# Matmuls of one width in groups, one PSUM tile per bank, and each weight load split in one piece, in a float32 decoder layer

## The chip, the cores and the metric

The kernel runs on one core of a Trainium2 chip. The metric is device time in microseconds (us) of one execution. TensorE (PE in the profile) multiplies and accumulates into PSUM, whose eight banks hold 512 float32 columns each. VectorE (DVE) and ScalarE (ACT) work on SBUF and PSUM. SyncE (SP) issues the DMAs that bring the weights from HBM.

## The reference

One decoder layer in float32, for 256 tokens of width 2048. All six modulation vectors come from `silu(c) @ w_ada + b_ada`. The part in front is attention of two kinds; the part behind it is a gated feed-forward network with a causal convolution over tokens, 43 x 128 = 5504 wide:

```
sh1, sc1, g1, sh2, sc2, g2 = split(silu(c) @ w_ada + b_ada, 6)
h      = rmsnorm(x, norm1_g) * (1 + sc1) + sh1
proj   = h @ w_in                                  # q, k, v of 8 + 8 heads, and an indexer's q, k, weights
o_sb   = stick_breaking_attention(q_sb, k_sb, v_sb)
o_ds   = sparse attention over the 64 keys that the indexer selects
x      = x + g1 * (concat(rmsnorm(o_sb), rmsnorm(o_ds)) @ w_out)
h2     = rmsnorm(x, norm2_g) * (1 + sc2) + sh2
u      = h2 @ w_up                                 # 2048 -> 2 * 5504
uc     = conv_b + sum over i of shift(u, 2 - i) * conv_w[i]
x      = x + g2 * ((silu(gate) * val) @ w_down)    # gate, val: the halves of uc
out    = rmsnorm(x, final_norm_g)
```

## The kernel before, in words

All weights stream through SBUF once, in loads of 128 x 2048 float32 (1 MB, `load`, line 135, four `raw` buffers). Every operand of a large matmul is split in a high part, rounded to fp32r (ACT, line 145), and a low part, the difference (DVE, line 146). `split` does this in pieces of 1024 columns, two for each load; the high and the low pieces have three buffers each (tags `wh` and `wl`). A product is then high x high + high x low + low x high, in one of three helpers:

- `nat` (lines 149 to 153): the activations are stationary, three matmuls of up to 512 columns. Used for the projections A, A2 (tiles B) and V.
- `trn` (lines 161 to 165): the weights are stationary, three matmuls of 256 columns. Used for QK, O and the first eight tiles of U.
- `fold` (lines 155 to 159): the weights are stationary and the activations' two parts lie side by side, so one matmul of 512 columns with the high weights writes the two products next to each other in one bank, and one of 256 columns adds the low weights' product to the second half. Used for U from tile `G0` = 8 on and for W. The two halves are added afterwards.

The stages in order: A (`do_A`), A2, V and QK for the first half of the contraction; A and A2 for the second; attention, with V and QK of the second half among it; O (`do_O`, w_out) with the residual and its squares; r2 and `h2_make`; U (`do_U`, w_up, f = 0 to 42, each in two loads i = 0, 1, each load with gate and value, `gv`); W (w_down, 43 loads). For f < 8 the first loads of all eight are taken before the second ones, since the later half of h2 isn't there yet. Behind each f of U follows the work on uc (lines 835 to 855); behind each k of W the residual (lines 871 to 877: DVE's lines 875 and 726 read the bank).

Columns of the modulation are made on the side by `ada` (lines 213 to 218: a load, and one DVE instruction of 2048 elements at line 215) or, in five groups, by TensorE (`ada_pe`). `pump` puts them between other work by a plan written out as digits.

In U and W the PSUM pool has 4 tiles of two banks each (`banks`, line 782). For f >= 8 such a tile holds gate and value of one f; for f < 8 it holds two f (lines 795 to 797); in W it holds k and k + 1 (lines 868 to 870). The framework orders each engine's instructions by its own planning ahead of the run, keeps track of who writes and reads each tile, and places semaphore waits accordingly; `order` adds an ordering by hand (lines 801 to 804: two splits come after the last residual).

Of the kernel before, what the change touches and what calls it, by code (L numbers as in the profile page):

```python
# [10 lines left out]
F32 = mybir.dt.float32  # L11
# [43 lines left out]
def layer(ctx: ExitStack, tc: tile.TileContext, a, out):  # L55
# [9 lines left out]
    def s2(shape, dt, name):  # L65
        return wp.tile(shape, dt, name=name, tag="s2", bufs=4)
# [331 lines left out]
    def do_A(pi):  # L398
# [6 lines left out]
        for j in range(PARTS[pi]):  # L405
            k = P0[pi] + j
            need(16 + k)
            need(k)
            w = load(a["wA"][k], 2048, f"wA{k}")
            h_make(k, pi, j)  # L410
            pump()
            for p_ in range(2):
                wh, wl = split(w, p_ * 1024, 1024, f"wA{k}{p_}")
                for c in range(2):
                    for t in range(NT):
                        nat(acc[2 * p_ + c][t], hp(hh, pi, j)[:, t * P:(t + 1) * P], hp(hl, pi, j)[:, t * P:(t + 1) * P],
                            wh[:, c * 512:(c + 1) * 512], wl[:, c * 512:(c + 1) * 512], j == 0, j == PARTS[pi] - 1)
# [7 lines left out]
    def natural(pi, src, width, per_load, acc, name):  # L425

        n = PARTS[pi]
        for k0 in range(0, n, per_load):
# [3 lines left out]
            for k1 in range(0, nk, 2):  # L432
                n2 = min(2, nk - k1)
                wh, wl = split(w, k1 * width, n2 * width, f"{name}{k0}{k1}")
                for jj in range(n2):
                    j = k0 + k1 + jj
                    for t in range(NT):
                        nat(acc[t][:, 0:width], hp(hh, pi, j)[:, t * P:(t + 1) * P], hp(hl, pi, j)[:, t * P:(t + 1) * P],
                            wh[:, jj * width:(jj + 1) * width], wl[:, jj * width:(jj + 1) * width], j == 0, j == n - 1)
# [13 lines left out]
    def do_QK(pi, h):  # L453
        n = PARTS[pi]
        acc = ps(f"QK{pi}{h}", tag=ptag[0])
        if n <= 8:
            w = load(a[f"wQK_{pi}"][h], 2 * n * P, f"wQK{pi}{h}")
        for p_ in range(2):
            o = p_ * n * P
            if n > 8:  # L460
                w = load(a[f"wQK_{pi}"][h][:, o:o + n * P], n * P, f"wQK{pi}{h}{p_}")
                o = 0
            for j0 in range(0, n, 8):
                nj = min(8, n - j0)
                wh, wl = split(w, o + j0 * P, nj * P, f"wQK{pi}{h}{p_}{j0}")
                for j in range(j0, j0 + nj):
                    trn(acc[:, p_ * S:(p_ + 1) * S], hp(hh, pi, j), hp(hl, pi, j),
                        wh[:, (j - j0) * P:(j - j0 + 1) * P], wl[:, (j - j0) * P:(j - j0 + 1) * P], j == 0, j == n - 1)
# [308 lines left out]

# [175 lines left out]
```

## Time and profile before

| what | value |
| --- | --- |
| median of 3 runs | 1251.4 us (1251.29 to 1252.37) |
| the profiled execution | 1258.62 us, of which its span (first to last instruction) 1256.8 us |
| mean granted TensorE clock | 0.979 |
| TensorE matmuls | 7120, busy 93% of the span |
| TensorE weight loads | 7120, busy 81% (beside matmuls) |
| DVE | 1232 instructions, busy 70% |
| ACT | 969 instructions, busy 50% |
| DMA | 303.48 MB, mean 241 GB/s |

Busy time of TensorE contains the overlap of matmuls that follow each other, so the distance between two starts tells more than the duration of one. A line can be that of a helper: 158 and 159 are `fold`, and the tile's name (U, W) tells who called it. Idle time in front of an instruction is shown in brackets with the instruction that ended it.

### The profile page before, as it was taken

How to read it: one execution, taken by the hardware profiler on the slowest of the kernel's cores; microseconds unless marked ns; L12 is line 12 of the kernel's file. 1: busy time of each engine (PE TensorE's matmuls, PEld its weight loads, DVE VectorE, ACT ScalarE, POOL GpSimd, SP SyncE). 2: the span in 40 equal slices, each digit the busy share in tenths (PEclk: the TensorE clock that was granted, in tenths of full speed). 3: DMA queues.
4: the chain of work that ended last, by engine and by line, in shares of the span. 5: the costliest groups of instructions: out<-in, count | busy, mean ns of one | idle time of the engine just before them, and what ended most of it. 6: DMA issues, size and time to landing. Idle time of an engine off the chain costs nothing.

```text
span 1256.8 us, 17813 instructions
## 1 busy us (share of the span) xinstructions
PE 1171.3 (93%) x7120; PEld 1016.9 (81%) x7120; DVE 880.5 (70%) x1232; ACT 629.3 (50%) x969; POOL 0.2 (0%) x4
## 2 busy tenths in 40 slices
PE   4699999899999997988999999999999999999995
PEld 2478987567879997987888888888888888888885
DVE  4877787789667888756789778777777645545443
ACT  3355554466555544454555555555555543443441
POOL 0000000000000000000000000000000000000000
PEclk9799999999999998999999999999999999999998
DMA  8988989667678896844578666666665445455431
GB/s 307 365 332 303 339 331 336 231 252 277 228 293 351 298 330 258 306 165 168 181 250 316 224 226 229 215 241 224 214 225 190 179 172 192 172 175 183 179 135 67
DMA packets 43282, 303.48 MB, mean 241 GB/s; under 512 B 4928, under 2 KB 5440, under 8 KB 7232
## 3 DMA queue, kind: packets, MB, share of 16 engines
q1 hardware_dynamic: 43200, 302.35, 66.0%
q8 instruction: 55, 0.90, 0.3%
q14 instruction: 27, 0.22, 0.0%
HBM read 300.24 MB, written 2.10 MB: 241 GB/s over the span
## 4 chain that ended last, share of the span: by engine, by line
PE 82%; DVE 11%; ACT 3%; DMA 2%; issue 2%; SPq 0%; DVEq 0%; ACTq 0%
PE U L158 20%; PE W L158 13%; PE U L159 10%; PE W L159 6%; DVE wa L215 3%; PE U L165 2%; PE U L164 2%; PE U L163 2%; PE O L165 2%; PE O L163 2%; PE O L164 2%; PE QK L163 2%; PE QK L164 2%; PE QK L165 2%; DMA wa<-wa 2%; PE A L151 2%
## 5 line engine op out<-in xcount | busy, mean ns | idle before, releaser
L215 DVE SCALAR_TENSOR_TENSOR wa<-wa,scb 128x2048 f32<-128x2048 f32 x76 | 173.5, 2285 | 6.9 <-DMA wa<-wa 6.6
L847 DVE SCALAR_TENSOR_TENSOR uc<-u,par,uc 128x254 f32<-128x254 f32 (+1 forms) x140 | 58.2, 478 | 0.0
L843 ACT ACTIVATE uc<-u,par 128x256 f32<-128x256 f32 x70 | 38.2, 593 | 0.8 <-DVE u L837 0.8
L854 ACT CAST aT<-uc 128x256 fp32r<-128x256 f32 x43 | 17.4, 404 | 28.8 <-DVE uc L853 28.7
L313 ACT ACTIVATE amul<-mod,b,par 128x1 f32<-128x1 f32 x32 | 12.0, 385 | 32.2 <-DVE wa L215 32.2
L192 PE MATMUL ap<-wg,csil 128*32 128x512 f32 x160 | 26.4, 679 | 0.3 <-DVE mod L201 0.3
L855 DVE TENSOR_TENSOR aT<-uc,aT 128x256 fp32r<-128x256 f32 x43 | 18.2, 422 | 10.0 <-ACT aT L854 9.9
L837 DVE TENSOR_TENSOR u<-U,u 128x512 f32<-128x512 f32 x35 | 23.9, 684 | 0.0
L316 ACT ACTIVATE mod<-mod,par 128x1 f32<-128x1 f32 x32 | 8.6, 302 | 27.5 <-DVE wa L215 26.6
L836 ACT COPY u<-U 128x512 f32<-128x512 f32 x35 | 20.3, 580 | 0.0
L853 DVE TENSOR_TENSOR uc<-uc 128x256 f32<-128x256 f32 x43 | 18.1, 420 | 1.5 <-ACT uc L849 0.7
L849 ACT ACTIVATE uc<-uc 128x256 f32<-128x256 f32 x43 | 17.7, 411 | 1.5 <-DVE uc L847 1.5
L731 ACT ACTIVATE x2q<-x1T 128x256 f32<-128x256 f32 x15 | 6.2, 415 | 21.3 <-DVE x1T L726 21.2
L875 DVE SCALAR_TENSOR_TENSOR x1T<-W,mod,x1T 128x256 f32<-128x256 f32 x16 | 7.7, 481 | 12.0 <-PE W L159 12.0
L847 DVE SCALAR_TENSOR_TENSOR uc<-U,par,uc 128x255 f32<-128x255 f32 (+1 forms) x32 | 14.5, 477 | 1.4 <-ACT uc L843 1.2
L192 PEld LDWEIGHTS ap<-wg,csil 128*32 128x32 f32 x160 | 4.7, 120 | 10.0 <-issue 8.2
L843 ACT ACTIVATE uc<-U,par 128x256 f32<-128x256 f32 x16 | 9.0, 561 | 7.5 <-DVE uc L847 7.5
L676 ACT ACTIVATE sbt<-sbt 128x384 f32<-128x384 f32 x8 | 4.2, 524 | 14.8 <-DVE sbt L675 14.8
L562 DVE SCALAR_TENSOR_TENSOR scw<-rl,wix,scw 128x128 f32<-128x128 f32 (+1 forms) x28 | 10.4, 409 | 0.0
L545 PE MATMUL rel<-ws,qixT 64*128 64x128 f32 (+1 forms) x64 | 8.5, 345 | 2.0 <-ACT rl L550 2.0
L273 PE MATMUL cb<-ident,csil 128*128 128x128 f32 x16 | 3.6, 422 | 7.1 <-DMA ident<-ident 7.1
L197 ACT COPY rw<-ap 128x512 f32<-128x512 f32 x5 | 2.9, 586 | 14.0 <-PE ap L192 13.3
(2810 smaller groups left out, 4600.7 us busy)
## 6 DMA issues: line engine op xcount, KB each, us to landing
wU<-wU SPq DMA_DIRECT2D x86, 1024.0 KB, 4.8
wa<-wa SPq DMA_DIRECT2D x76, 1024.0 KB, 5.4
wD<-wD SPq DMA_DIRECT2D x43, 1024.0 KB, 4.6
wg<-wg SPq DMA_DIRECT2D x20, 1024.0 KB, 6.2
wA<-wA SPq DMA_DIRECT2D x16, 1024.0 KB, 6.4
wQK<-wQK SPq DMA_DIRECT2D x16, 1024.0 KB, 6.9
wO<-wO SPq DMA_DIRECT2D x16, 1024.0 KB, 6.9
xT<-xT SPq DMA_DIRECT2D x4, 512.0 KB, 5.9
```

The source lines that it names most:

```text
L151: T.matmul(pt, lhsT=xh, rhs=wh, start=first, stop=False)
L158: T.matmul(pt, lhsT=wh, rhs=x, start=first, stop=False)
L159: T.matmul(pt[:, 1, :], lhsT=wl, rhs=x[:, 0, :], start=False, stop=last)
L163: T.matmul(pt, lhsT=wh, rhs=xh, start=first, stop=False)
L164: T.matmul(pt, lhsT=wh, rhs=xl, start=False, stop=False)
L165: T.matmul(pt, lhsT=wl, rhs=xh, start=False, stop=last)
L192: T.matmul(pt[32 * j:32 * j + 32, :], lhsT=csil[:, k:k + 1].to_broadcast([P, 32]), rhs=w[:, j * 512:(j + 1) * 512], start=q == 0, stop=q == 3)
L215: i = V.scalar_tensor_tensor(out=w, in0=w, scalar=1.0, in1=scb, op0=ALU.mult, op1=ALU.mult, accum_out=mod[:, j:j + 1])
L836: A.copy(out=u, in_=acc[:, :, 1, :])
L837: V.tensor_tensor(out=u, in0=acc[:, :, 0, :], in1=u, op=ALU.add)
L843: A.activation(uc[:, gv, :], u[:, gv, :], AF.Identity, scale=par[:, PCW + 3 * i + 2:PCW + 3 * i + 3], bias=par[:, PCB + i:PCB + i + 1])
L847: V.scalar_tensor_tensor(out=uc[:, gv, sft:S], in0=u[:, gv, 0:S - sft], scalar=par[:, o:o + 1], in1=uc[:, gv, sft:S], op0=ALU.mult, op1=AL ...
```

## The change

It does four things. `fold` takes a list of steps and issues all their 512-column matmuls with the high weights first and all 256-column matmuls with the low weights after them; U and W hand it eight steps at a time. In U and W a PSUM tile is one bank (`bank`, 8 tiles): one per f for f < 8, one each for gate and value for f >= 8, one per k in W, where the residual's work is issued after the group of eight in which k ends. `split` handles a whole load of up to 2048 columns, with two buffers each for the high and the low part. To make room the tag `s2` has 3 buffers in place of 4, and the sum u has a tag of its own with 2. The two orderings by hand become one: the whole split of the first load of U comes after the last residual.

```diff
-        return wp.tile(shape, dt, name=name, tag="s2", bufs=4)
+        return wp.tile(shape, dt, name=name, tag="s2", bufs=3)
...
-    def split(w, off, n, name):
-        wh = wp.tile([P, 1024], F32R, name=name + "h", tag="wh", bufs=3)
-        wl = wp.tile([P, 1024], F32R, name=name + "l", tag="wl", bufs=3)
-        lo_[1] = A.copy(out=wh[:, 0:n], in_=w[:, off:off + n])
-        lo_[0] = V.tensor_tensor(out=wl[:, 0:n], in0=w[:, off:off + n], in1=wh[:, 0:n].bitcast(F32), op=ALU.subtract)
+    def split(w, n, name):
+        wh = wp.tile([P, 2048], F32R, name=name + "h", tag="wh", bufs=2)
+        wl = wp.tile([P, 2048], F32R, name=name + "l", tag="wl", bufs=2)
+        lo_[1] = A.copy(out=wh[:, 0:n], in_=w[:, 0:n])
+        lo_[0] = V.tensor_tensor(out=wl[:, 0:n], in0=w[:, 0:n], in1=wh[:, 0:n].bitcast(F32), op=ALU.subtract)
...
-    def fold(pt, x, wh, wl, first, last):
-        T.matmul(pt, lhsT=wh, rhs=x, start=first, stop=False)
-        T.matmul(pt[:, 1, :], lhsT=wl, rhs=x[:, 0, :], start=False, stop=last)
+    def fold(steps):
+        for pt, x, wh, _, first, _ in steps:
+            T.matmul(pt, lhsT=wh, rhs=x, start=first, stop=False)
+        for pt, x, _, wl, _, last in steps:
+            T.matmul(pt[:, 1, :], lhsT=wl, rhs=x[:, 0, :], start=False, stop=last)
...
     def do_O(acc, m, s, xh, xl):
         w = load(a["wO"][m, s], 2048, f"wO{m}{s}")
+        wh, wl = split(w, 2048, f"wO{m}{s}")
         for p_ in range(2):
-            wh, wl = split(w, p_ * 1024, 1024, f"wO{m}{s}{p_}")
             for j in range(8):
...
-    pool3 = ctx3.enter_context(tc.tile_pool(name="psC", bufs=4, space=PSUM))
+    pool3 = ctx3.enter_context(tc.tile_pool(name="psC", bufs=8, space=PSUM))
...
-    def banks(name):
-        return pool3.tile([P, 2, 2, S], F32, name=name, tag="ps", bufs=4)
+    def bank(name):
+        return pool3.tile([P, 2, S], F32, name=name, tag="ps", bufs=8)
...
         if i == 0:
-            if f >= G0:
-                uacc[f] = banks(f"U{f}")
-            elif f % 2 == 0:
-                t_ = banks(f"U{f}")
-                uacc[f], uacc[f + 1] = t_[:, 0], t_[:, 1]
+            uacc[f] = [bank(f"U{f}{gv}") for gv in range(2)] if f >= G0 else bank(f"U{f}")
         w = load(a["wU"][f, i], 2048, f"wU{f}{i}")
+        wh, wl = split(w, 2048, f"wU{f}{i}")
+        if (f, i) == (0, 0):
+            order(lo_[0], resid_i[0])
+            order(lo_[1], resid_i[1])
         for gv in range(2):
-            wh, wl = split(w, gv * 1024, 1024, f"wU{f}{i}{gv}")
-            if (f, i, gv) in ((0, 0, 1), (1, 0, 0)):
-                order(lo_[0], resid_i[0])
-                if gv == 0:
-                    order(lo_[1], resid_i[1])
+            steps = []
...
                 if f >= G0:
-                    fold(uacc[f][:, gv], x, wh[:, sl], wl[:, sl], k == 0, k == KT - 1)
+                    steps.append((uacc[f][gv], x, wh[:, sl], wl[:, sl], k == 0, k == KT - 1))
...
+            fold(steps)
...
         if f >= G0:
-            u = s2([P, 2, S], F32, f"u{f}")
-            A.copy(out=u, in_=acc[:, :, 1, :])
-            V.tensor_tensor(out=u, in0=acc[:, :, 0, :], in1=u, op=ALU.add)
+            u = wp.tile([P, 2, S], F32, name=f"u{f}", tag="u2", bufs=2)
+            for gv in range(2):
+                A.copy(out=u[:, gv, :], in_=acc[gv][:, 1, :])
+                V.tensor_tensor(out=u[:, gv, :], in0=acc[gv][:, 0, :], in1=u[:, gv, :], op=ALU.add)
...
+    wacc = {}
     for q in range(FT):
         w = load(a["wD"][:, q * 2048:(q + 1) * 2048], 2048, f"wD{q}")
+        wh, wl = split(w, 2048, f"wD{q}")
         for p_ in range(2):
-            wh, wl = split(w, p_ * 1024, 1024, f"wD{q}{p_}")
-            for j in range(8):
-                k, f = divmod((2 * q + p_) * 8 + j, FT)
-                if f == 0 and k % 2 == 0:
-                    acc = banks(f"W{k}")
-                fold(acc[:, k % 2], aT[f // 4][:, f % 4, :, :], wh[:, j * P:(j + 1) * P], wl[:, j * P:(j + 1) * P],
-                     f == 0, f == FT - 1)
+            steps, done = [], None
+            for j in range(8 * p_, 8 * p_ + 8):
+                k, f = divmod(16 * q + j, FT)
+                if f == 0:
+                    wacc[k] = bank(f"W{k}")
+                sl = slice(j * P, (j + 1) * P)
+                steps.append((wacc[k], aT[f // 4][:, f % 4, :, :], wh[:, sl], wl[:, sl], f == 0, f == FT - 1))
                 if f == FT - 1:
...
+                    done = k
+            fold(steps)
+            if done is not None:
...
```

The loops of A, A2, V and QK change in the same way as `do_O`: one `split` per load, and the same matmuls in the same order.

## Rows read from the trace of the kernel before

**Rows 1.** The page: busy time by engine, and the chain's shares by line.
```profile
PE 1171.3 (93%) x7120; PEld 1016.9 (81%) x7120; DVE 880.5 (70%) x1232; ACT 629.3 (50%) x969; POOL 0.2 (0%) x4
...
PE U L158 20%; PE W L158 13%; PE U L159 10%; PE W L159 6%; DVE wa L215 3%; PE U L165 2%; PE U L164 2%; PE U L163 2%; PE O L165 2%; PE O L163 2%; PE O L164 2%; PE QK L163 2%; PE QK L164 2%; PE QK L165 2%; DMA wa<-wa 2%; PE A L151 2%
```

**Rows 2.** Stages: length; PE, PEld, DVE, ACT, POOL busy (count); PEclk, DMA share, GB/s.
```profile
372.00:472.00 100.00, 99.15 (x814) 95.33 (x807) 82.81 (x97) 51.15 (x77) 0.00 (x0) 1.00 0.86 321
531.00:595.00 64.00, 54.50 (x405) 52.22 (x404) 39.72 (x61) 30.61 (x47) 0.00 (x0) 0.95 0.51 181
595.00:988.00 393.00, 392.73 (x2224) 340.24 (x2223) 302.05 (x414) 219.35 (x313) 0.00 (x0) 1.00 0.63 225
988.00:1243.00 255.00, 243.51 (x1379) 210.49 (x1379) 123.90 (x135) 104.72 (x120) 0.00 (x0) 1.00 0.45 161
```

**Rows 3.** Timeline of PE in U: start, duration; the first of eight pairs, twice.
```profile
801.74 0.40 PE L158 MATMUL U<-h,wU2610h 128*128 128x512 f32 x1
...
804.57 0.40 PE L158 MATMUL U<-h,wU2611h 128*128 128x512 f32 x1
```

**Rows 4.** Timeline of PE in V: eighteen steps of 512 columns lie between.
```profile
119.83 0.39 PE L153 MATMUL V<-V0140h,hl 128*128 128x512 f32 x1
...
123.91 0.39 PE L153 MATMUL V<-V0142h,hl 128*128 128x512 f32 x1
```

**Rows 5.** Timeline of PE in O: twenty-four steps of 256 columns lie between.
```profile
420.27 0.28 PE L163 MATMUL O<-osh,wO310h 128*128 128x256 f32 x1
...
423.15 0.28 PE L163 MATMUL O<-osh,wO311h 128*128 128x256 f32 x1
```

**Rows 6.** Waits from 988 to 1243 us: total us, times, longest.
```profile
PEld W L158 <- DVE x1T L726: 13.8, 8, 2.5
...
PE W L158 <- DVE x1T L726: 11.5, 8, 2.2
```

**Rows 7.** Timeline of DVE at the first of these waits.
```profile
1003.65 1.23 DVE L146 TENSOR_TENSOR wD31l<-wD,wD31h 128x1024 fp32r<-128x1024 f32 x1 [1.65 <-ACT wD31h L145]
...
1005.31 0.48 DVE L726 SCALAR_TENSOR_TENSOR x1T<-W,mod,x1T 128x256 f32<-128x256 f32 x1
```

**Rows 8.** Timeline of PE in U's second pass (tiles are named wU, f, i, gv).
```profile
531.26 0.28 PE L163 MATMUL U<-h,wU010h 128*128 128x256 f32 x1
...
538.20 0.39 PE L163 MATMUL U<-h,wU210h 128*128 128x256 f32 x1 [1.02 <-ACT wU210h L145]
...
594.86 0.40 PE L158 MATMUL U<-h,wU801h 128*128 128x512 f32 x1
```

**Rows 9.** Timelines of ACT and DVE in O.
```profile
426.15 1.05 ACT L145 CAST wO410h<-wO 128x1024 fp32r<-128x1024 f32 x1 [1.82 <-PE O L164]
...
428.50 1.22 DVE L146 TENSOR_TENSOR wO410l<-wO,wO410h 128x1024 fp32r<-128x1024 f32 x1
...
431.61 2.28 DVE L215 SCALAR_TENSOR_TENSOR wa<-wa,scb 128x2048 f32<-128x2048 f32 x1
```

**Rows 10.** The page's groups: busy us, mean ns of one, idle before and its releaser.
```profile
L215 DVE SCALAR_TENSOR_TENSOR wa<-wa,scb 128x2048 f32<-128x2048 f32 x76 | 173.5, 2285 | 6.9 <-DMA wa<-wa 6.6
L855 DVE TENSOR_TENSOR aT<-uc,aT 128x256 fp32r<-128x256 f32 x43 | 18.2, 422 | 10.0 <-ACT aT L854 9.9
L836 ACT COPY u<-U 128x512 f32<-128x512 f32 x35 | 20.3, 580 | 0.0
L847 DVE SCALAR_TENSOR_TENSOR uc<-U,par,uc 128x255 f32<-128x255 f32 (+1 forms) x32 | 14.5, 477 | 1.4 <-ACT uc L843 1.2
```

**Rows 11.** The chain in order of time at two starts, O and U: start, us.
```profile
389.36 0.95 ACT wO200h L145
390.33 1.24 DVE wO200l L146
...
474.60 1.23 DVE wU100l L146
```

**Rows 12.** Line 215 alone from 20 to 531 us: busy us, two records each.
```profile
20.00:531.00 511.00, 137.47 (x120) 0.96 0.81 300
```

More of the change, by code (lines that the diff above doesn't have):

```diff
@@ L411, in do_A @@
             pump()
[L412 to L417, printed above, removed]
+            wh, wl = split(w, 2048, f"wA{k}")
+            for c in range(4):
+                sl = slice(c * 512, (c + 1) * 512)
+                for t in range(NT):
+                    nat(acc[c][t], hp(hh, pi, j)[:, t * P:(t + 1) * P], hp(hl, pi, j)[:, t * P:(t + 1) * P], wh[:, sl],
+                        wl[:, sl], j == 0, j == PARTS[pi] - 1)
         for g in range(4):
@@ L431, in natural @@
             pump()
[L432 to L439, printed above, removed]
+            wh, wl = split(w, nk * width, f"{name}{k0}")
+            for jj in range(nk):
+                j = k0 + jj
+                for t in range(NT):
+                    nat(acc[t][:, 0:width], hp(hh, pi, j)[:, t * P:(t + 1) * P], hp(hl, pi, j)[:, t * P:(t + 1) * P],
+                        wh[:, jj * width:(jj + 1) * width], wl[:, jj * width:(jj + 1) * width], j == 0, j == n - 1)
     def do_A2(pi):
@@ L455, in do_QK @@
         acc = ps(f"QK{pi}{h}", tag=ptag[0])
-        if n <= 8:
-            w = load(a[f"wQK_{pi}"][h], 2 * n * P, f"wQK{pi}{h}")
+        w = load(a[f"wQK_{pi}"][h], 2 * n * P, f"wQK{pi}{h}")
+        wh, wl = split(w, 2 * n * P, f"wQK{pi}{h}")
         for p_ in range(2):
[L459 to L468, printed above, removed]
+            for j in range(n):
+                sl = slice((p_ * n + j) * P, (p_ * n + j + 1) * P)
+                trn(acc[:, p_ * S:(p_ + 1) * S], hp(hh, pi, j), hp(hl, pi, j), wh[:, sl], wl[:, sl], j == 0, j == n - 1)
         dst = qk[h // 4]
@@ L701, in do_O @@
         w = load(a["wO"][m, s], 2048, f"wO{m}{s}")
+        wh, wl = split(w, 2048, f"wO{m}{s}")
         for p_ in range(2):
-            wh, wl = split(w, p_ * 1024, 1024, f"wO{m}{s}{p_}")
             for j in range(8):
-                trn(acc[:, p_ * S:(p_ + 1) * S], xh[:, j, :], xl[:, j, :], wh[:, j * P:(j + 1) * P],
-                    wl[:, j * P:(j + 1) * P], s == 0 and p_ == 0 and j == 0, s == 1 and p_ == 1 and j == 7)
+                sl = slice((8 * p_ + j) * P, (8 * p_ + j + 1) * P)
+                trn(acc[:, p_ * S:(p_ + 1) * S], xh[:, j, :], xl[:, j, :], wh[:, sl], wl[:, sl],
+                    s == 0 and p_ == 0 and j == 0, s == 1 and p_ == 1 and j == 7)
     acc = [ps(f"O{m}", tag="acc") for m in range(4)]
@@ L776, in layer @@
     ctx3 = ExitStack()
-    pool3 = ctx3.enter_context(tc.tile_pool(name="psC", bufs=4, space=PSUM))
-    psum_pool[0] = (pool3, {"ps": 4})
+    pool3 = ctx3.enter_context(tc.tile_pool(name="psC", bufs=8, space=PSUM))
+    psum_pool[0] = (pool3, {"ps": 8})
     ptag[0] = "ps"
-    def banks(name):
-        return pool3.tile([P, 2, 2, S], F32, name=name, tag="ps", bufs=4)
+    def bank(name):
+        return pool3.tile([P, 2, S], F32, name=name, tag="ps", bufs=8)
     aT = []
@@ L807, in do_U @@
                 x = h2[k // 4][:, k % 4, :, :]
-                sl = slice(j * P, (j + 1) * P)
+                sl = slice((8 * gv + j) * P, (8 * gv + j + 1) * P)
                 if f >= G0:
-                    fold(uacc[f][:, gv], x, wh[:, sl], wl[:, sl], k == 0, k == KT - 1)
+                    steps.append((uacc[f][gv], x, wh[:, sl], wl[:, sl], k == 0, k == KT - 1))
                 else:
```

12 lines of the change are left out of this document (7 added, 5 removed).

## The prediction

> **What bounds the kernel now.** The shares of busy time come first [rows 1]: TensorE is busy 93% of the 1256.8 us, and the chain that ended last lies on it for most of its length, above all in `fold` (lines 158 and 159, in U and W). So the next view is the table by stage, where the question is how much of each stage TensorE does *not* work [rows 2]. Three stretches differ. From 595 to 988 us (U, tiles f = 8 to 42) it is busy without a gap, so only shorter matmuls can help. From 988 to 1243 (W) it lacks 11.5 us, and from 531 to 595 (second half of U's first eight tiles) 9.5 us, at a mean clock of 0.95; there waits can be removed. From 372 to 472 (O), as in the other stages of `nat` and `trn`, it is full, and DVE with 82.8 us of 100 stands close behind it: here a change of DVE's or ACT's order can only hurt.
>
> Last comes the distance from start to start of matmuls, since busy time hides their overlap. In `fold` a pair of 512 and 256 columns takes 2.83 us / 8 = 0.3538 us [rows 3]. Where only 512 columns follow each other it is 4.08 / 18 = 0.2267 us each [rows 4]; where only 256, 2.88 / 24 = 0.1200 us [rows 5]. One of each would be 0.3467 us. The pair costs 7 ns more than its two halves in uniform rows (6 to 7, as the stamps are rounded).
>
> **The change part by part.**
>
> **1. Grouping.** `fold` issues 8 wide matmuls, then 8 narrow ones. There are 35 x 32 = 1120 pairs in U and 43 x 16 = 688 in W, 1808 together. If the 7 ns belong to the alternation, seven of eight disappear: 1808 x 7/8 x 6.6 ns = 10.5 us. Nothing lies beside them: in this stretch TensorE has no gap [rows 2]. Bounds: 0, if the price stays with the widths and not the order, and 12.8 (1808 x 7.1 ns, no transition left). I take 10.5, since [rows 4, 5] are the same types, with a weight load ahead of every matmul, as in `fold` (7120 of each on the page). The Trainium skill (TensorE: Matmul & The Clock Gate, Back-to-back issue gap) gives a matmul a gap that depends on its own columns alone, N/2.4 + 2.5 ns, and no price for a change of width; by it, called an estimate, a pair is 325 ns in either order and the term is 0. The cadences above lie higher and the pair is not the sum of its halves, so the trace doesn't bear that out; what it would do here is rival A.
>
> **2. One tile per bank in W.** Before, k and k+1 share a tile of two banks. TensorE waits 8 times, 11.5 us in all, for DVE's line 726 [rows 6], always at the first matmul of an odd k, which goes to the other bank of a tile that DVE is still reading. Before DVE gets there it does a split already queued, then the two reads, 0.48 us each [rows 7]. With a tile per k and 8 of them this wait has no cause: the bank that k+1 gets was emptied several k earlier. W holds 688 x 0.3538 = 243.4 us of matmuls in 255, which gives the same: 11.5. With the restart of the pipeline I take 12.0 (bounds 11.5 and 13.8, the wait of the weight loads). What is late next: nothing near; each k lasts 43 x 0.35 = 15 us and its two reads may fall anywhere in it. The tail behind the last k stays as it is.
>
> **3. One tile per bank in U, f < 8.** Here f and f+1 share a tile; TensorE takes f = 2, 4, 6, 8 ahead of f = 1, 3, 5, 7, whose split isn't made yet when it comes [rows 8] (f = 2 there; three more of the kind, at 4, 6 and 8). From 531.26 to 594.86 us there are 16 pieces of 24 x 0.12 = 2.88 us and one of 2.83 in `fold`, 48.9 us, in 63.6: 14.7 us are lost, part of it in waits like the 1.0 us at wU210h, part at the lowered clock that follows some of them (mean 0.95 of the stretch). With a tile per f the order is f = 0, 1, 2, ... and no matmul waits for a reader. DVE needs per f a split of 2.3 us and about 2.8 us of small work behind U (four at line 847 of 0.48, two like line 855 of 0.42 [rows 10]), under the 5.76 us of TensorE, but not by much. I take 13 (bounds 8, with half a microsecond or more of new wait per f, and 14.7).
>
> **4. One split of 2048.** An ACT copy of 1024 takes 1.05 us, a DVE subtraction 1.22 [rows 9]; of 2048, DVE 2.28 (line 215, the same number of elements), ACT 1.05 + 2 x (1.05 - 0.58) = 1.99 by the slope from 512 [rows 9, 10]. Per load ACT saves 0.1 and DVE 0.15 us; TensorE sets the pace, so that is worth nothing. Two things are paid.
>
> *At each start*, where TensorE stands ready and the split is the last to come, the first matmul pair could go 1.05 + 1.22 us after the copy began; now 1.99 + 2.28: +2.0 us, less where TensorE waits for something else too. In `fold` it is nothing: the 8 wide matmuls (1.8 us) need the copy alone and cover most of the subtraction. Starts in `nat` and `trn` that the chain shows: the first loads of A and its last ones (wA60), the end of A's second part, V and QK behind attention, wO200, and U's first load (the last two stand in [rows 11]). In U it is worse, as the whole split of load 0 must now come behind the last residual, and DVE's small steps to r2 queue behind 2.28 us in place of 1.23. I set A 1.5, A's second part 1.5, V and QK together 1.5, O 2, U 2: 8.5 us (bounds 2, if other waits cover them, and 14, seven full ones).
>
> *In steady running* the reserve shrinks. A buffer is free when TensorE has left it (the copy's releaser in [rows 9]). With three of 1024 it is needed again after 2 x 2.88 us and takes 1.05 + 1.22: 3.5 us in hand. With two of 2048 it is needed after 5.76 and takes 4.3: 1.5 us (1.1 in `nat`, whose load lasts 24 x 0.2267 = 5.44). What can eat it is line 215, 2.3 us in one piece on DVE, 60 of them up to 531 us [rows 12] beside 68 loads. DVE is idle while ACT copies, so a line 215 whose data has landed begins there, ahead of the subtraction, and ends in time; one that starts just before the copy ends makes TensorE wait 2.3 - 1.5 = 0.8 us. I take 2 us, two or three such (bounds 0 and 12). In `fold` the copy's buffer is free 8 x 0.12 us before the load ends and the subtraction's result is needed 1.8 us into the next: 4 us in hand, no cost. The Trainium skill (Perfetto Trace Analysis, Optimizing Scalar/DVE Operations) speaks against this part: where ScalarE and VectorE aren't saturated but cause bubbles elsewhere, it advises breaking instructions up. The start rows agree; no row here shows it yet for steady running.
>
> **5. The rest** is set at nothing. s2 with 3 buffers and u2 with 2 of its own: U's chain had four for u and uc, now two and three. Loads: a raw buffer is held for 4.3 us instead of one piece of TensorE and a split; SP's queue keeps its order. If either cover fails it shows as waits of ACT or SP, inside the bounds of part 4.
>
> **The sum**, against the profiled execution: -10.5 - 12.0 - 13 + 8.5 + 2 = -25.0 us, 1256.8 to 1231.8 of span. The profiled execution itself took 1258.6; the median of the runs is 1251.4, and I take the difference as the same there: 1226.4.
>
> **The rivals.**
>
> A. *Alternation isn't the cause* of the 7 ns, grouping moves nothing: 1226.4 + 10.5 = 1237. For it: no row shows a group inside `fold`. Against: two uniform cadences whose sum is less than the pair.
>
> B. *The tiles change nothing*: the waits in W and U come from reads as such, a matmul into any bank waits behind DVE. Then 12 and 13 us stay: 1251.4. Against it: all 8 waits stand at odd k and none at even k, whose tile is new.
>
> C. *Slower: two buffers starve TensorE.* Place: A to O and U's first tiles, DVE between ACT's copy and its subtraction. Price: 0.9 us for each line 215 that lands late enough to start there (0.8 and the restart). With 40 of the 60 it is 36 us, in place of the 2: 1226.4 + 34 = 1260. It makes the kernel slower from about 30 on (25 + 2 = 27 us / 0.9). For it: O's loads run at 321 GB/s [rows 2], and line 215 waits for its data already, 6.6 us in all [rows 10]. Against it: DVE's idle time, while ACT copies, now lies just where a line 215 fits.
>
> **How the numbers follow.** Forecast 0.70; A 0.15; B 0.05; C 0.07; 0.03 for something unseen, a third of it on each side and within. The forecast's own bounds: best -12.8 - 13.8 - 14.7 + 2 = -39; all at once is unlikely, -38 gives 1213. Worst without C: -5 - 11.5 - 8 + 14 + 4 = -6.5, 1245; I end at 1243. That range, 1213 to 1243, takes in A and leaves out B, C and little else. Faster by over 0.2% (2.5 us, about what a measurement of this kernel can tell from no change): forecast, A and a third of the unseen, 0.86. Same, B and a third: 0.06. Slower, C and a third: 0.08.
>
> **What would show it.** Grouping: starts 0.227 us apart in rows of 8 on line 158's successor, then 0.120. W: no wait of TensorE for DVE's reads, 43 x 16 pairs in 239 us. U: f in order and a clock of 1.00 between the first pass and f = 8. Splits: 1.99 and 2.28 us, TensorE's new waits for ACT or DVE at the starts named, and in O a subtraction ending some 1.4 us ahead of its first use. Wrong would be a cadence of 0.354 in groups (A), waits for DVE's reads that remain (B), or gaps of about 0.8 us load after load between 100 and 530 us (C).

## The result, and the profile after

The changed kernel takes 1233.6 us (median of 4 runs, 1232.9 to 1235.3), beside 1251.4 for the kernel before in the same batch of runs. The ratio is 0.9862, with a 95% interval of 0.9845 to 0.9879: 17.8 us faster. The forecast was 1226.4 with a range of 1213 to 1243; the time lies inside, 7 us above the forecast. The profiled execution took 1232.9 us, 1230.9 of it span, 25.9 less than that of before. The forecast for the span was 1231.8. That this agrees so closely is partly luck, as the terms below show.

The page of the kernel after, the line that answers to the first of [rows 1]:

```profile
PE 1159.2 (94%) x7120; PEld 1017.6 (83%) x7120; DVE 871.2 (71%) x1078; ACT 605.6 (49%) x815; POOL 0.2 (0%) x4
```

As many matmuls as before, 12.1 us less busy time, and 154 instructions fewer each on DVE and ACT. The stages say more. The kernel after by stage, columns as in [rows 2] (length; PE, PEld, DVE, ACT, POOL busy; PEclk, DMA share, GB/s): O, U's first pass, U's second pass, the rest of U, W.

```profile
372.00:478.00 106.00, 97.06 (x774) 94.33 (x773) 78.82 (x81) 44.09 (x62) 0.00 (x0) 0.95 0.75 275
478.00:540.00 62.00, 51.81 (x404) 51.01 (x403) 50.10 (x61) 27.66 (x38) 0.00 (x0) 0.89 0.72 265
540.00:586.00 46.00, 45.74 (x381) 45.53 (x380) 35.32 (x47) 27.25 (x36) 0.00 (x0) 1.00 0.58 205
586.00:977.00 391.00, 391.00 (x2241) 344.09 (x2241) 309.84 (x387) 220.32 (x282) 0.00 (x0) 1.00 0.63 229
977.00:1218.00 241.00, 241.00 (x1386) 212.18 (x1384) 117.90 (x93) 95.18 (x77) 0.00 (x0) 1.00 0.47 170
```

The last three are full: the second pass, 63.6 us before with one piece of `fold` (2.8) in it, takes 46.6 (539.78 to 586.42, start of its first matmul to that of `fold`), and W, 255.0 before, takes 240.1. The first of them is not: in O, which was full in [rows 2], TensorE now lacks 9 us of 106, and its clock is 0.95: from 400.4 to 410.7 us, around the waits at rsbb and osh below, the granted clock is 0.50, the lower of its two levels (1.2 GHz).

The groups stand as intended. Timeline of PE in the kernel after (start, duration; rows with a count join matmuls that follow each other):

```profile
800.56 1.12 PE L162 MATMUL U<-h,wU270l 128*128 128x256 f32 x8
801.51 2.00 PE L160 MATMUL U<-h,wU270h 128*128 128x512 f32 x8
803.35 0.76 PE L162 MATMUL U<-h,wU270l 128*128 128x256 f32 x5
```

From 800.56 to 801.51 eight narrow ones go by in 0.95 us, from 801.51 to 803.35 eight wide ones in 1.84: 2.79 for eight pairs, where [rows 3] give 2.83.

Waits of PE in the kernel after, 372 to 540 us (total us, times, longest):

```profile
PE r2b L129 <- DVE r2y L126: 5.9, 1, 5.9
PE rsbb L129 <- DVE rsby L126: 4.7, 1, 4.7
PE O L166 <- ACT osh L640: 2.8, 1, 2.8
PE U L166 <- DVE g L305: 2.7, 1, 2.7
```

Before, the same stretch has neither a wait at rsbb nor one at osh, and the one at r2b is 1.7 us. From 586 to 1218 us TensorE waits for nothing at all; the eight waits of [rows 6] are gone.

So where did it go? The table gives, for the kernels of the experiments below too, the start of TensorE's first or last matmul of a stretch, in us from the start of the span. "Heads" is the last matmul of the stick-breaking heads, "rsb" the first one of their norm.

| | before | p12 | after | e6 | e5 | e7 | e8 | e9 |
| --- | --- | --- | --- | --- | --- | --- | --- | --- |
| A, second part, first | 170.2 | 170.8 | 172.5 | 168.6 | 175.8 | 173.2 | 168.9 | 169.8 |
| attention, last `av` | 290.0 | 290.3 | 295.1 | 293.2 | 297.0 | 294.6 | 291.9 | 291.7 |
| heads, last | 379.9 | 376.4 | 389.8 | 373.9 | 391.9 | 389.5 | 373.7 | 372.2 |
| rsb | 383.3 | 379.9 | 398.1 | 394.6 | 400.1 | 391.8 | 382.9 | 381.4 |
| O, last | 472.0 | 468.4 | 478.2 | 476.3 | 480.3 | 474.5 | 464.2 | 462.7 |
| U, first | 479.0 | 475.4 | 490.2 | 487.6 | 488.3 | 486.6 | 472.5 | 471.0 |
| U, first pass, last | 531.1 | 523.7 | 539.7 | 536.0 | 539.8 | 536.5 | 523.1 | 521.8 |
| W, first | 988.3 | 961.0 | 977.5 | 973.3 | 977.6 | 974.4 | 960.4 | 957.6 |

From before to after: 6.2 us are lost up to O's end and 5.1 more up to U's first matmul; the first pass of U gains 2.8, from there to W it is 19.3 (14.1 of it in the second pass), in W 14.9. Two executions with one order of instructions differ by some us before U (e5 and after are the same up to there, and lie 3.3 us apart at A's second part), so the early rows are read with that in mind.

### The profile page after: what moved, and what is told of

Its sections match the earlier page's. It is cut to its first block, busy times and chain, and to the rows that moved or that the text cites. A ratio compares the mean times of both kernels' runs of the same rounds, so it can differ in the third digit from the quotient of the medians.

```text
span 1230.9 us, 17235 instructions
## 1 busy us (share of the span) xinstructions
PE 1159.2 (94%) x7120; PEld 1017.6 (83%) x7120; DVE 871.2 (71%) x1078; ACT 605.6 (49%) x815; POOL 0.2 (0%) x4
## 4 chain that ended last, share of the span: by engine, by line
PE 85%; DVE 8%; ACT 3%; DMA 3%; issue 2%; SPq 0%; DVEq 0%; ACTq 0%
PE U L160 21%; PE W L160 13%; PE U L162 11%; PE W L162 7%; PE O L168 2%; PE O L167 2%; PE O L166 2%; PE U L168 2%; PE U L166 2%; PE U L167 2%; PE QK L168 2%; PE QK L166 2%; PE QK L167 2%; PE A L152 2%; PE A L153 2%; PE A L151 2%
## 5 line engine op out<-in xcount | busy, mean ns | idle before, releaser
L839 DVE SCALAR_TENSOR_TENSOR uc<-u,par,uc 128x255 f32<-128x255 f32 (+1 forms) x140 | 67.4, 482 | 31.1 <-ACT uc L835 27.8
L835 ACT ACTIVATE uc<-u,par 128x256 f32<-128x256 f32 x70 | 42.1, 602 | 87.8 <-DVE u L829 87.8
L828 ACT COPY u<-U 128x256 f32<-128x256 f32 x70 | 25.6, 366 | 56.1 <-PE U L162 56.1
L829 DVE TENSOR_TENSOR u<-U,u 128x256 f32<-128x256 f32 x70 | 29.2, 417 | 0.0
L721 DVE SCALAR_TENSOR_TENSOR x1T<-O,mod,xT 128x256 f32<-128x256 f32 x16 | 7.0, 478 | 13.0 <-PE O L168 13.0
L151 PE MATMUL A<-wA0h,hh 128*128 128x512 f32 x8 | 3.7, 536 | 9.0 <-ACT hh L311 9.0
```

The lines of the kernel that those rows point to most:

```text
L151: T.matmul(pt, lhsT=xh, rhs=wh, start=first, stop=False)
L828: A.copy(out=u[:, gv, :], in_=acc[gv][:, 1, :])
L829: V.tensor_tensor(out=u[:, gv, :], in0=acc[gv][:, 0, :], in1=u[:, gv, :], op=ALU.add)
L835: A.activation(uc[:, gv, :], u[:, gv, :], AF.Identity, scale=par[:, PCW + 3 * i + 2:PCW + 3 * i + 3], bias=par[:, PCB + i:PCB + i + 1])
L839: V.scalar_tensor_tensor(out=uc[:, gv, sft:S], in0=u[:, gv, 0:S - sft], scalar=par[:, o:o + 1], in1=uc[:, gv, sft:S], op0=ALU.mult, op1=AL ...
```

## The experiments

The theories: mine, that the four terms add up as in the sum; rivals A, B and C; and, once the result was known, three places in which the split of 2048 could cost what steady running doesn't.

**The parts one by one.** p1 is the grouping on the kernel before, with tiles of two banks kept; p2 is the tile per bank, with the old `fold`; p3 is the split of 2048 with its two buffers, `s2` and `u2`; p12 is p1 and p2 together.

```diff
 p1, in W:
+                    wacc[k] = banks(f"W{k}") if k % 2 == 0 else wacc[k - 1]
...
+            fold(steps)
+            if done is not None:
 p2:
-            if f >= G0:
-                uacc[f] = banks(f"U{f}")
-            elif f % 2 == 0:
-                t_ = banks(f"U{f}")
-                uacc[f], uacc[f + 1] = t_[:, 0], t_[:, 1]
+            uacc[f] = [bank(f"U{f}{gv}") for gv in range(2)] if f >= G0 else bank(f"U{f}")
...
-                if f == 0 and k % 2 == 0:
-                    acc = banks(f"W{k}")
+                if f == 0:
+                    acc = bank(f"W{k}")
 p3:
-        wh = wp.tile([P, 1024], F32R, name=name + "h", tag="wh", bufs=3)
-        wl = wp.tile([P, 1024], F32R, name=name + "l", tag="wl", bufs=3)
+        wh = wp.tile([P, 2048], F32R, name=name + "h", tag="wh", bufs=2)
+        wl = wp.tile([P, 2048], F32R, name=name + "l", tag="wl", bufs=2)
```

p1: 

> Grouping alone on the kernel before: splits of 1024 with three buffers and the tiles of two banks stay. The theory (the price of the alternation is real, but part of it returns at the first five wide matmuls of each group: 27 ns in each of 226 groups) expects 6.7 us less, 1244.7, and groups of 1.85 us wide and 0.95 us narrow. The prediction's own term was 10.5 us less, 1240.9. Rival A (the order doesn't matter) expects no change, 1251.4. The waits for DVE's reads in W (8) and the lost 14 us in U's second pass stay in every theory.

p2: 

> One tile per bank in U and W alone: wide and narrow matmuls alternate as before, splits of 1024 with three buffers. The theory (shared tiles are the whole cause of both waits) expects 12 us less in W and 13 to 14.5 less in U's second pass, 25 to 26.5 us in all, 1225 to 1226.5. Rival (the profiled execution of the kernel before was slower than its usual ones in these stages, so that there is less to take away) expects 17 to 20 less, 1231 to 1234. Rival B (the tiles change nothing) expects 1251.4.

p3: 

> The split of 2048 with two buffers each alone (with the smaller s2 and the tag u2): tiles of two banks and alternating matmuls as before. The theory (the price is paid at the small chains of DVE in front of O's second half and of U, and in A, as the profile after shows: 8.5 us at the start of U's second pass) expects 8.5 us more, 1260. The rival that the three parts don't add, and that the price of the split alone is what the medians lack (6.7 + 26 - 17.8 = 15 us), expects 1266. The forecast's reading that the steady reserve of 1.5 us is enough expects no gaps of TensorE load after load between 100 and 470 us.

p12: 

> Grouping and one tile per bank together, splits of 1024 with three buffers: the change without its third part. If the split costs 8.5 us in the medians too, 1233.6 - 8.5 = 1225; if it costs 15 us, 1218.6 (1251.4 less 6.7 less 26); if the split pays for itself, since both engines have fewer instructions, 1233.6 or more. U's second pass lasts 46 to 47 us and W 240 us in every theory.

| kernel | median us | ratio to before | 95% interval |
| --- | --- | --- | --- |
| p1, grouping alone | 1260.8 | 1.0050 | 1.0032 to 1.0068 |
| p2, tiles alone | 1223.5 | 0.9735 | 0.9702 to 0.9769 |
| p3, split alone | 1289.6 | 1.0272 | 1.0242 to 1.0301 |
| p12, grouping and tiles | 1218.0 | 0.9708 | 0.9684 to 0.9732 |

Before is 1254.1 in this batch. Grouping alone is *slower*, by 6.7 us, which no theory expected. The largest wait of PE in W, in p1, and behind it W's window:

```profile
PE W L157 <- DVE x1T L726: 17.4, 8, 2.2
```

```profile
980.20:1247.60 267.40, 249.96 (x1379) 218.10 (x1378) 122.91 (x134) 104.40 (x120) 0.00 (x0) 0.97 0.45 154
```

The eight waits of [rows 6] grow from 11.5 to 17.4 us, and the clock falls to 0.97 in a stage where it was 1.00; W takes 267.4 us instead of 255.0. With the group, the reads of tile k come behind all of its group, by which time TensorE already stands at k + 1 in the other bank of the same tile. In U from the second pass on, p1 does gain: 450.4 us instead of 456.9. The grouping's worth thus hangs on the tiles, and a part's price read with the other parts absent is not its price in the change.

p2 shows the tiles alone. Stages of p2 (second pass, rest of U, W; columns as above):

```profile
522.60:568.70 46.10, 46.10 (x386) 46.10 (x385) 37.23 (x58) 28.54 (x44) 0.00 (x0) 1.00 0.62 220
568.70:964.40 395.70, 395.70 (x2242) 343.01 (x2241) 313.58 (x453) 222.44 (x350) 0.00 (x0) 1.00 0.63 226
964.40:1207.50 243.10, 243.10 (x1378) 210.92 (x1377) 123.42 (x135) 104.02 (x120) 0.00 (x0) 1.00 0.50 169
```

All three are full at a clock of 1.00, with no wait left. W goes from 255.0 to 243.1: 12 us. The second pass, 60.8 us before without its piece of `fold`, takes 46.1. Rival B falls.

Stages of p12, the same two behind the second pass:

```profile
570.00:961.00 391.00, 391.00 (x2241) 344.28 (x2241) 311.39 (x454) 224.03 (x352) 0.00 (x0) 1.00 0.64 229
961.00:1201.00 240.00, 240.00 (x1377) 211.32 (x1376) 122.83 (x134) 103.54 (x119) 0.00 (x0) 1.00 0.50 171
```

Beside p2 that is 4.7 us in U and some 3 in W, 7.6 by the first and last matmuls (684.8 to 677.2 us): the grouping itself, where TensorE is full on both sides. The medians differ by 5.4 us, but their intervals overlap, and two of p2's six runs, at 1214.9, lie below all of p12's; here the cadence is the better witness. Rival A falls too, though not by the whole amount.

And p12 holds everything of the change but the split, with its buffers and its ordering: 1218.0 against 1233.6. Given the other parts, the split costs 15.6 us in the medians and 16.3 in the spans (19 by the ratios, as after and p12 ran in different batches). Alone, in p3, it costs 35.5, more than any theory expected. p3's span is 29.4 us longer than that of before; 10.2 of them lie ahead of U, as in the kernel after, and 13.9 between the start of U's second pass and W: there the shared tiles make TensorE take f = 2, 4, 6, 8 ahead, whose splits are now twice as long. Waits of PE in p3 from 540 us on, the two largest of U, and behind them the second pass's window:

```profile
PE U L164 <- DVE wU61l L146: 2.9, 1, 2.9
PE U L162 <- ACT wU61h L145: 2.8, 1, 2.8
```

```profile
542.90:618.40 75.50, 58.70 (x410) 56.20 (x409) 37.46 (x52) 28.28 (x38) 0.00 (x0) 0.89 0.38 139
```

75.5 us, some matmuls of f = 8 among it, for a pass that takes 46 elsewhere: for 16.8 of them TensorE stands idle, and the clock is 0.89.

**Where the split costs its 16 us.** Three mends on the kernel after, each for one suspected place. e6: the instructions go back to 1024 columns, in the same two buffers of 2048. e5: r2's small DVE steps go ahead of U's first splits. e7: the norm of the stick-breaking heads (rsb) is written behind the second instead of the fourth of O's first loads.

```diff
 e6, in split:
...
+        for o in range(0, n, 1024):
+            e = min(o + 1024, n)
+            lo_[1].append(A.copy(out=wh[:, o:e], in_=w[:, o:e]))
+            lo_[0].append(V.tensor_tensor(out=wl[:, o:e], in0=w[:, o:e], in1=wh[:, o:e].bitcast(F32), op=ALU.subtract))
 e5, in U (after[0] is r2's last DVE step):
-            order(lo_[0], resid_i[0])
+            order(lo_[0], after[0])
             order(lo_[1], resid_i[1])
+        if (f, i) == (1, 0):
+            order(lo_[0], after[0])
+            order(lo_[1], after[0])
 e7, in O:
-    for m in range(4):
+    for m in range(2):
         do_O(acc[m], m, 0, odh, odl)
         pump()
 ... (the norm, rsb)
+    for m in range(2, 4):
+        do_O(acc[m], m, 0, odh, odl)
+        pump()
```

e6: 

> The changed kernel with the same two buffers of 2048 for each part, but each split issued as two ACT copies and two DVE subtractions of 1024. The theory (the split costs its 16 us because small instructions of serial chains queue behind blocks of 1.9 and 2.3 us) expects most of it back: first matmul of U 8 to 12 us earlier, 1220 to 1225. The rival (two buffers in place of three, so the rotation, is what costs) expects the changed kernel's 1233.6, within 2.

e5: 

> The changed kernel with two orderings more: the subtractions of U's first two loads, and the copy of the second, come after the last step of r2. The theory (3.8 us of the 6.1 us gap ahead of r2's broadcast is DVE's two subtractions and ACT's second copy standing among r2's steps) expects U's first matmul 3 to 5 us earlier and 1229 to 1231. The rival (the later subtraction only moves the wait to U's first matmul) expects 1233.6.

e7: 

> The changed kernel, with the norm of the stick-breaking heads (its two small TensorE steps, the chain to rsb and the split of the heads) written down behind the second of O's first four loads instead of behind the fourth. The theory (8 us of TensorE's time in O go because the order runs all of O's first loads before the norm's chain, so that nothing is left to hide it) expects the waits of 4.9 and 3.2 us around rsb to vanish and 1228 to 1230. The rival (DVE and ACT are simply too full there, wherever the chain stands) expects the waits elsewhere and 1233.6.

e6 takes 1227.4 us, ratio 0.9787 (0.9761 to 0.9813): 6.2 us under the kernel after, and not the 1220 to 1225 that was expected; U's first matmul comes 2.6 us earlier, not 8 to 12. The buffers are as few and as large as in after, so what is gained comes from the shorter instructions and from what the planned order makes of them. It shows at A's second part (172.5 to 175.8 us in after, e5 and e7, 168.6 to 169.8 in e6, e8 and e9). The heads' last matmul comes 16 us earlier, but 10 of them are order alone: ahead of it on TensorE's queue stand 124 of O's matmuls in after and 40 in e6, 0.12 us each. This is what a block of 2048 does to a head's chain of short steps (start, us, in the kernel after):

```profile
380.51 0.50 ACT L661 ACTIVATE sbt<-z 128x384 f32<-128x384 f32 x1
...
380.89 1.90 ACT L145 CAST wO20h<-wO 128x2048 fp32r<-128x2048 f32 x1
...
382.68 0.54 ACT L662 ACTIVATE sbt<-sbt 128x384 f32<-128x384 f32 x1
...
382.82 2.29 DVE L146 TENSOR_TENSOR wO20l<-wO,wO20h 128x2048 fp32r<-128x2048 f32 x1 [2.30 <-ACT wO20h L145]
...
383.38 0.52 ACT L663 ACTIVATE sbt<-sbt 128x384 f32<-128x384 f32 x1
...
385.03 0.55 DVE L664 SCALAR_TENSOR_TENSOR sbt<-z,sbt 128x384 f32<-128x384 f32 x1
...
385.87 0.81 PE L666 MATMUL u<-sbt,cst 128*128 128x384 f32 x2
```

The head's step at line 661 ends at 381.01, the next, at 662, starts at 382.68, behind the copy for O. Its step on DVE (line 664) has its input at 383.90 and starts at 385.03, behind the subtraction: 2.8 us of this head's chain in all. TensorE meanwhile works on O's earlier loads and stands 1.0 us, for wO20l.

Of the 16 us only 1.8 are left at O's end, and the waits behind the heads stay. Waits of PE in e6 from 365 to 540 us:

```profile
PE r2b L129 <- DVE r2y L126: 5.0, 1, 5.0
PE rsbb L129 <- DVE rsby L126: 4.0, 1, 4.0
PE O L169 <- ACT osh L643: 2.8, 1, 2.8
PE U L169 <- DVE g L308: 2.8, 1, 2.8
PE O L170 <- DVE osl L644: 2.6, 1, 2.6
```

In after they are 5.9, 4.7, 2.8, 2.7 and 0.5 us. So the length is the smaller part of the price; the larger is the order of the queues, which the framework plans ahead of the run. Timeline of PE at rsb, in p12 and then in after; the norm is written behind O's fourth load in both:

```profile
386.77 0.28 PE L165 MATMUL O<-odh,wO101l 128*128 128x256 f32 x1
386.89 0.38 PE L129 MATMUL rsbb<-ident,rsby 128*128 128x128 f32 x2
387.03 0.36 PE L163 MATMUL O<-odh,wO200h 128*128 128x256 f32 x1
```

```profile
397.95 0.28 PE L168 MATMUL O<-odh,wO30l 128*128 128x256 f32 x1
398.07 0.50 PE L115 MATMUL rsbp<-nones,ws 128*128 128x1 f32 x4
403.25 0.66 PE L129 MATMUL rsbb<-ident,rsby 128*128 128x128 f32 x2 [4.68 <-DVE rsby L126]
```

In before and p12 the norm's first step, rsbp, stands behind 48 of O's matmuls and rsbb behind 96, so that 48 of them cover the chain between the two. In after and e6 both stand behind 192, all of the first four loads, and nothing covers it. On DVE it is alike: between r2p's last matmul and r2's steps stands one subtraction of 1.2 us in before and p12; ahead of those steps and among them stand two of 2.3 in after and four of 1.2 in e6. Why the planning puts them so with two buffers of 2048 is not shown.

e5 takes 1231.4, ratio 0.9819 (0.9795 to 0.9843), an interval that ends where that of after begins. DVE between O and U, in the kernel after and then in e5 (start, us, in brackets the idle time before):

```profile
481.68 2.29 DVE L146 TENSOR_TENSOR wU00l<-wU,wU00h 128x2048 fp32r<-128x2048 f32 x1 [2.33 <-ACT wU00h L145]
483.88 0.15 DVE L121 TENSOR_SCALAR r2v<-r2p 128x2 f32<-128x2 f32 x1
483.95 2.28 DVE L146 TENSOR_TENSOR wU10l<-wU,wU10h 128x2048 fp32r<-128x2048 f32 x1
486.15 0.15 DVE L124 SCALAR_TENSOR_TENSOR r2l<-r2y 128x2 f32<-128x2 f32 x1
...
486.53 0.16 DVE L126 SCALAR_TENSOR_TENSOR r2y<-r2l,r2y 128x2 f32<-128x2 f32 x1
```

```profile
483.94 0.16 DVE L121 TENSOR_SCALAR r2v<-r2p 128x2 f32<-128x2 f32 x1 [2.49 <-ACT r2l L119]
...
484.57 0.16 DVE L126 SCALAR_TENSOR_TENSOR r2y<-r2l,r2y 128x2 f32<-128x2 f32 x1
484.65 2.28 DVE L146 TENSOR_TENSOR wU00l<-wU,wU00h 128x2048 fp32r<-128x2048 f32 x1
```

In after one subtraction stands ahead of r2's four steps on DVE and one among them: from the last matmul of r2p to the first of r2b it is 6.1 us, in e5 2.1. With r2 ahead, U's first matmul comes 8.0 us behind O's last one instead of 12.1. The first pass then lasts 51.5 us instead of 49.4, since the subtractions are now late themselves: half of the 4 us comes back as another wait. From O's last matmul to the end of that pass it is 59.5 us instead of 61.5, and the medians differ by 2.2.

e7 takes 1230.8, ratio 0.9821 (0.9794 to 0.9848), 2.8 us under after, where the intervals overlap by a hair. With 41 of O's matmuls now between rsbp and rsbb the 4.7 us wait there is gone; the 2.8 at osh stays.

**All three mends together** (e8), and the kernel before once more, for the spread of a trace.

e8: 

> The changed kernel with three things at once: splits in instructions of 1024 in the same two buffers, r2's steps ahead of the first subtractions of U, and the norm behind the second of O's loads. If these three are what the split of 2048 costs (6.2, 2.2 and 4 to 5 us), they add up to 13 and give 1220; the kernel with grouping and tiles alone, at 1218.0, would then be explained to within 2. If the rotation of two buffers costs by itself, 1224 or more.

before, again: 

> The kernel before itself, for a second profile. Its runs spread from 1248.7 to 1259.3, and the first profile was of one of 1258.6. The theory (the spread comes from DMA waits of line 215 and its like in single places) expects the same order of instructions and the same cadences, with differences of some us in one or two stretches up to U's second pass; U's second part and W agree within 0.5 us.

e8 takes 1215.1 us, ratio 0.9687 (0.9661 to 0.9714): 18.5 us under after, where the three alone give 6.2, 2.2 and 2.8, 11.2 together. By the ratios, though, each to before in its own batch, the three give 9, 5 and 5 us and e8 22, so the times don't show that the mends help each other. The traces do: O's last matmul comes 1.8 us earlier with e6, 3.6 with e7, and 13.9 with all three. With the heads early (e6) *and* rsb not queued behind the fourth load (e7), enough of O's matmuls stand behind rsb's steps to cover them. Waits of PE in e8 from 365 to 540 us:

```profile
PE U L169 <- DVE g L308: 2.8, 1, 2.8
PE r2b L129 <- DVE r2y L126: 2.0, 1, 2.0
PE r2p L115 <- ACT x1q L732: 1.0, 1, 1.0
PE aq L206 <- ACT rw L203: 0.7, 1, 0.7
PE U L171 <- DVE wU10l L149: 0.4, 1, 0.4
```

No rsbb, no osh, and 2.0 at r2b, about as before. e8's O:

```profile
365.00:464.00 99.00, 98.25 (x807) 95.82 (x802) 80.83 (x96) 47.07 (x76) 0.00 (x0) 1.00 0.87 321
```

O is as full as in [rows 2], with two buffers of 2048, and the whole is not measurably different from p12 with its three of 1024. From 586 us on the kernel after itself already goes at p12's pace (391.0 us in U, 240.1 in W, in both). From A to QK (57 to 372 us) TensorE's waits for a load's split are 4.4 us in all in after, 4.1 in p12. So the rotation of two buffers costs nothing that these runs can tell, and rival C falls. What the split cost was in part its length, at places where something short waits behind it (e6), and for the larger part the place of two short chains in the queues, which e7 and e5 put right by hand. That order was not run on p12; p12's waits from 365 to 540 us are 5.6 us in all, e8's 6.9.

The second trace of before has a span of 1254.5, not 1256.8: U's first matmul 1.6 us earlier, W 253.9 us instead of 255.0, the second pass with all of `fold` 457.5 instead of 456.9. Terms under 2 us can't be read from one pair of traces.

**Groups of sixteen.** What is left of a change of width? g16 is p12 with both pieces of a load in one group of 16; g16_r2 is g16 with the first subtraction of U's second load behind r2's last step; e9 is e8 with groups of 16.

```diff
 g16, in U:
+        steps = []
         for gv in range(2):
-            steps = []
...
-            fold(steps)
+        fold(steps)
```

g16: 

> Grouping and one tile per bank with splits of 1024 in three buffers, as in the run of these two, but in groups of sixteen, a whole load. If each change of width costs a group 25 ns net (five wide matmuls of 228 to 236 in place of 226.7, one narrow of 114), halving 226 groups gives 2.8 us: 1215. If the price is spread over every wide matmul, no change: 1218.

g16_r2: 

> Groups of sixteen, one tile per bank, splits of 1024 in three buffers, and the first subtraction of U's second load behind r2's last step. The theory (r2's three steps wait 1.2 us for it) expects 1 us less than with groups of sixteen alone, 1215.8; the rival (it only moves) 1216.8. A difference this small is likely to stay inside the interval.

e9: 

> The changed kernel with the three mends together (instructions of 1024, r2's steps first, the norm behind the second of O's loads) and groups of sixteen. If the effects add, 1215.1 less the 1.2 us that groups of sixteen gave on the other kernel: 1213 to 1214, and U's fold and W some 2 us shorter together than with groups of eight. If a group of sixteen holds the high weights' buffer too long for two buffers of 2048, TensorE waits for ACT in U and W and it is 1215 or more.

g16 takes 1216.8, ratio 0.9697 (0.9672 to 0.9723), 1.2 us under p12 with overlapping intervals; e9 takes 1212.2, ratio 0.9666 (0.9638 to 0.9694), 2.8 us under e8, which overlaps as well. By its median e9 is the fastest kernel of this study: 41.9 us under its runs of before (1254.1), where the change has 17.8. Timeline of PE in g16:

```profile
800.80 2.00 PE L157 MATMUL U<-h,wU2810h 128*128 128x512 f32 x8
802.64 1.98 PE L157 MATMUL U<-h,wU2811h 128*128 128x512 f32 x8
804.46 1.11 PE L159 MATMUL U<-h,wU2810l 128*128 128x256 f32 x8
```

The first eight of the sixteen take 1.84 us to the next start, as in groups of eight, the second eight 1.82 (0.2275 each): the slow ones stand at the head of a group. Half as many heads save some 1 to 3 us, no more than the runs can tell. g16_r2 gives 1215.8, ratio 0.9690 (0.9660 to 0.9719), which can't be told from g16; in its trace U's first matmul comes 6.3 us behind O's last, in g16's 7.0, and the end of the first pass moves by 0.3. With splits of 1024 there is nothing to mend there.

## Why the prediction was right or wrong

| term | forecast us | measured us | where |
| --- | --- | --- | --- |
| 1 grouping | -10.5 | -7.6 | p12 beside p2, from U's second pass to W's end |
| 2 tiles in W | -12.0 | -12.0 | W in p2 beside before |
| 3 tiles in U, second pass | -13 | -14.7 | that pass, p12 beside before |
| tiles in U, first pass | 0 | -3.8 | 52.2 to 48.4 us, p12 beside before |
| 4 split, starts | +8.5 | +16.3 | span, after beside p12 |
| 4 split, steady running | +2 | 0 | after: no wait from 586 us on, in A to QK as in p12; e8 beside p12 |
| sum | -25.0 | -21.8 | |

**The signs of the terms** were right, and the order of the three gains: a gain from the tiles and the grouping, paid in part ahead of U. The price came out as the largest single term.

**Grouping: right in cause, mis-sized.** The step that failed is the assumption that a matmul in a group goes at the cadence of the uniform rows [rows 4, 5] at once. U's 1120 pairs take 395.7 us alternating (p2) and 391.0 in groups (p12): 353.4 and 349.2 ns each, where the forecast came to 348 (seven eighths of the way to 346.7). 1808 pairs by 4.2 ns are the 7.6 us. In the groups of eight (mean over `fold` in U, kernel after) the distances of the wide ones are 233, 236, 228, 232 and 231 ns for the first five and 226.7 for the rest, while the narrow ones take 119 in the mean; 8 x 2.5 = 20 ns per group are left, 226 times, 4.5 us. The Trainium skill (TensorE: Matmul & The Clock Gate, Back-to-back issue gap) has no price for a change of width; p12 beside p2 shows that there is one. Its rule, which it gives for a matmul by itself, makes a pair 325 ns as an estimate; the shortest pairs of any run here, in groups of sixteen (e9), take 347.9. Why five matmuls, not one, are slow behind a change of width stays open: no run here tells.

**Tiles in W: right** in mechanism, place and size (bounds 11.5 to 13.8). The rows carried it: eight waits, all at odd k [rows 6], and a sum of matmuls that left just so much [rows 2]. What the prediction didn't see is that grouping alone would have made these same waits longer (p1).

**Tiles in U: right**, -14.7 beside -13, at its upper bound; no new wait over 0.3 us per f came in its place, and the clock of the pass is 1.00. That the first pass gains 3.8 us as well (p12 beside before) the prediction left out: it read the second pass alone, though the tiles of two f bind both.

**The split: the steps named were the right places, two sizes were wrong.** Up to attention the forecast was A 1.5, A's second part 1.5, V and QK 1.5, 4.5 in all; the last `av` comes 4.8 us later in after than in p12 (6.7 in e5, with the same order, so a part of the agreement is luck). Behind it came 2 for O and 2 for U; measured are 5.0 more up to O's end, 5.1 up to U's first matmul, and 1.5 behind it. The working priced one full start, 2.0 us, for each: the added length of one block, met once, in a queue order that stays. That step failed. At O the price isn't paid by the first load: rsb's steps now stand behind four loads on TensorE's queue, and nothing is left that covers their chain, 4.7 and 2.8 us of waits; with instructions half as long (e6) it is 4.0 and 2.8. At U the prediction did say that r2's small steps would queue behind 2.28 us in place of 1.23, and counted this once; it was two such subtractions, wU00l and wU10l. So what was missed is how much splitting stands ahead of two short chains, which is a matter of the order in the queues more than of the length of a block.

The Trainium skill (Perfetto Trace Analysis, Optimizing Scalar/DVE Operations) advises breaking instructions up where ScalarE and VectorE aren't saturated but cause bubbles elsewhere. e6 agrees, with 6.2 of 15.6 us, on ACT 49% and DVE 71% busy; the rest needed the order changed too.

**Steady running: the forecast +2 was 0.** The reserve of 1.5 us, worked out from [rows 9, 10], was enough: no waits for a split load after load, in A to QK or behind 586 us. The lengths were close: the copy of 2048 takes 1.88 to 1.90 us (1.99 forecast), the subtraction 2.28 to 2.29 (2.28).

**From the traces to the median: the weak step.** The sum was made against one profiled execution, and the difference taken as the same at the median. The profiled execution of before took 1258.6 us, near the top of its runs; its median is 1251.4 in the runs shown and with the result, and 1253.7 to 1254.1 in the batches of the experiments. The terms as measured, -21.8, fit the latter: 1254.1 - 21.8 = 1232.3, beside 1233.6. Of the 7.2 us by which the forecast lay low, 3.2 are in the terms (+2.9 grouping, +5.8 split, -5.5 tiles), and 2.7 in what the median of before is taken to be; that 1251.4, of three or four runs, is the one that is off is likely and not shown. The span alone hit so well because 4.1 us between the two profiled executions belong to none of the terms (3.6 of them lie ahead of O's end, p12 beside before), about what the terms lack.

**The rivals.** A is refuted in its strong form, as the gain isn't 0, and holds for 2.5 of the 7 ns. B is refuted by p2's full W, C by the waits of the kernel after and by e8. The price that was missed, 16.3 us at the starts, lies above the forecast's own bound for them (14); the range holds the time since its worst case has 4 more for steady running, which cost nothing.

## What to carry to other kernels

Two banks in one tile are one object to the waits: if one is read while the other is written, give each its own tile, *before* anything is done that makes the reads later (grouping here cost 6.7 us without it and saved 5 to 8 with it). A longer instruction on an engine with time to spare cost nothing in steady running here, but short steps that share the engine wait behind it, and the planned order of the queues can change with it: look up what stands ahead of each short chain in every queue, and count that, not the starts of stages. And where several causes delay the same point, mend them together before judging one: e6 and e7 alone brought O's end 1.8 and 3.6 us forward, all three mends 13.9.

## What the runs showed of the hardware

- Matmuls with a weight load each follow each other at 226.7 ns (512 columns) and 120.0 ns (256) in uniform rows, 353.4 ns for a pair in alternation and 349.2 in groups of eight. Behind a change from 256 to 512 columns five wide matmuls in turn are 2 to 9 ns slower than 226.7; the first narrow one behind a wide one is 7 ns faster than 120.0 (113).
- TensorE's granted clock was 0.89 in p3's second pass, with waits of 1.8 to 2.9 us in it, and 1.00 in the same pass where it waited nowhere (p2, p12). In W with eight waits of 2.2 us in the mean it was 0.97 (p1) and with eight of 1.4 us 1.00 [rows 2, 6]. These are means over stretches at 1.2 and at 2.4 GHz.
- A copy of 2048 float32 columns to fp32r takes ACT 1.88 to 1.90 us, where two of 1024 in a row take 1.98 to 2.00 (e6, e8); the saving, 0.1 us per load, bought nothing here, as TensorE sets the pace.
